# A hybrid decoder trunk: whole blocks ahead of chunk products in linear attention, state updates in one run, and drains of plain sums without a wait for the combined ones

## The chip, the cores and the metric

The kernel runs on one core of a Trainium2 chip. Every time is in device microseconds (us) of that core, from the start to the end of one execution. The engines are named as the profile names them: PE is the matrix engine, PEld its loading of stationary operands, DVE the vector engine, ACT the scalar engine, POOL the general one, and SP the one that here only issues transfers.

## The reference, cut to what matters

Two layers work on 256 tokens of width 2048, all in float32. A layer has a linear-attention group of 8 heads and a stick-breaking group of 8 heads side by side, an output projection, and a squared-ReLU MLP of width 8192.

```
# linear attention, in chunks of 64 tokens: q_e = q exp(b), k_e = k exp(-b), b the summed log gates
scores  = where(causal, q_e k_e^T, 0)          # within a chunk
o_intra = scores v
u       = (k exp(b_last - b))^T v              # one per chunk
state   = decay * state + u                    # over chunks
o_inter = q_e state_before_the_chunk
o_gla   = rms_norm(o_intra + o_inter) * silu(gate)
# the rest of a layer
x = x + concat(o_gla, o_sb) w_o
x = x + square(relu(rms_norm(x) w_up)) w_down
```

## The kernel before, in words

**Products.** A product of float32 operands is made of three faster ones: each operand is split into a high and a low part (`act` for activations, `whi` and `wlo` for weights), and high by high, high by low and low by high are summed (lines 569 to 571, and 1352 to 1354). Weights arrive in tiles `raw` from HBM, ACT writes `whi` (lines 550 and 1239), DVE writes `wlo` (lines 552 and 1243). For two of the eight tiles of an MLP unit the low part is made by ACT and an adding transfer instead (`dlo`, lines 1249 and 1252).

**First half of a layer (projections and attention).** `unit` multiplies one block of 512 projection columns. Small work of the attention heads is hung on the units' steps with `after`: each step of a unit is 12 products, and work due after n steps is issued behind the n-th. The order within this half is then left to the scheduler of the language, which may also set instructions of one engine past each other.

For a pair e of linear-attention heads (4 pairs in each layer) there are two such pieces of work. `gla_pair` (line 988) makes six sums u of three chunks and two heads in one PSUM bank (line 996), four blocks of scores in another (line 1013), the states S of three chunks on DVE (lines 1002 and 1004), and the masked scores (line 1024). Two steps later `gla_out` (line 1031) sums, in one bank, four whole blocks of 128 by 128 (masked scores by values, line 1037) and six chunk products (scaled queries of 64 tokens by the state before the chunk, line 1049). The sums u, the scores and the chunk products have 64 output rows each, the upper or the lower half of the partitions; in the profile they are the matmuls with `128*64`, all others have `128*128`. Each of these plain float32 products stands in the profile as two matmul instructions.

**Second half (output projection and MLP).** From line 1072 on the work of a layer is given to a planner, `Plan`, as pieces with an engine, an assumed length and the pieces that they depend on. PE keeps the order in which pieces are added; a piece of DVE or ACT gets a due time from those who use it, and whichever is ready and due first comes next. What it writes out is the order on PE, DVE and ACT.

A unit of that half is one block of 1024 output columns: 16 times `up` and `down` in turns of two, and two of the output projection, in each layer. Four of its eight weight tiles (two in the output projection) are multiplied in a form with seven block products for eight. So of the eight PSUM banks a unit fills, four (m1, m5, m6, m7) hold sums that are to be combined, and four (m2, m4, m3, m8) hold **plain** sums, which only have to be added to the result. The result is `xb` (the residual stream) in a `down` unit and a tile `act` in an `up` unit. m1, m5, m6 and m7 are complete three steps before the unit's end, m2 and m4 one step before, m3 and m8 at its end. The next unit begins with m2 and m4 (six matmuls each), then m3 and m8.

`down_tail` (line 1360) and `up_tail` (line 1407) add the pieces that drain a unit's banks: `sums` combines the four banks of the first kind, `half` adds the plain banks, m2 and m4 in its first call and m3 and m8 in its second. All of the drains on DVE go through `combine` (line 1080). An `up` unit then goes through ReLU (ACT, line 1438), transposes on PE (line 1456) into m5, m7, m1 and m6, and squares (ACT, line 1463).

## Time and profile before

| what | value |
|---|---|
| median of 3 runs | 2174.51 us (2174.15 to 2175.42) |
| the profiled execution | 2175.34 us, of which the traced span is 2173.2 us |
| PE, busy share of the span | 99% |
| PEld | 82% |
| DVE | 85% |
| ACT | 67% |
| DMA queue with the weights, share of 16 engines | 54.8% |
| granted PE clock | 1.00 |

Matmuls are pipelined: each shows some 0.39 us in the timeline while the next starts 0.23 us later. So a busy PE says little, and costs are read from the distance between two starts. The linear attention stands at about 242 to 300 us in the first layer and 1319 to 1378 us in the second; the planned half at 307 to 1090 us and 1386 us to the end.

### The profile page before, as it was taken

The page shows a single profiled execution, that of the slowest core. Times are in us where ns is not written, and L with a number is a line of the kernel's source. Part 1 is how long each engine was busy: PE and PEld are TensorE (multiplying, and loading weights), DVE is VectorE, ACT ScalarE, POOL GpSimd, SP SyncE. Part 2 cuts the span into 40 slices and gives each one's busy share as a digit, 9 for nine tenths or more (in the row PEclk, how much of TensorE's full clock was granted, in tenths as well). Part 3 has the DMA queues.
Part 4 walks back from the last instruction along what each step waited for, and adds up shares of the span by engine and source line. Part 5 has one row for each costly group of instructions (what it writes and reads, how often), then busy time and mean ns, then how long its engine had stood idle before and what let it go on. Part 6 is the DMA issues. An engine that isn't in the chain of part 4 may idle for free.

```text
span 2173.2 us, 28234 instructions
## 1 busy us (share of the span) xinstructions
PE 2159.4 (99%) x10256; PEld 1784.1 (82%) x10256; DVE 1857.4 (85%) x2469; ACT 1456.6 (67%) x1855; POOL 152.0 (7%) x202
## 2 busy tenths in 40 slices
PE   9999999999999999999999999999999999999999
PEld 7988778888888888888888887788888888888887
DVE  5677569999999999999967775699999999999998
ACT  5555356687677677677745553567776776776775
POOL 0020000000000000000100200000000000000000
PEclk9999999999999999999999999999999999999999
DMA  6655455688888888888746544556888888888885
GB/s 226 193 163 159 155 174 195 196 250 251 249 256 236 262 249 241 260 246 251 230 139 195 173 156 152 195 177 219 247 251 264 234 257 248 246 243 251 258 245 175
DMA packets 171502, 476.15 MB, mean 219 GB/s; under 512 B 9210, under 2 KB 34370, under 8 KB 171364
## 3 DMA queue, kind: packets, MB, share of 16 engines
q1 hardware_dynamic: 152932, 407.24, 54.8%
q0 software_dynamic: 18432, 67.12, 16.4%
q8 instruction: 80, 1.31, 0.2%
q14 instruction: 58, 0.48, 0.1%
HBM read 405.12 MB, written 2.10 MB: 187 GB/s over the span
## 4 chain that ended last, share of the span: by engine, by line
PE 92%; DVE 4%; issue 2%; ACT 1%; DMA 1%; SPq 0%; POOL 0%; ACTq 0%
PE acc L569 6%; PE acc L571 6%; PE acc L570 6%; PE acc L616 3%; DVE act L1080 2%; PE acc L620 1%; DVE wlo L1243 1%; ACT whi L1239 1%; PE ps L1037 1%; PE ps L1049 1%; DMA dlo<-raw 1%; DVE t L1080 0%; PE ps L996 0%; PE ps L732 0%; PE ps L678 0%
## 5 line engine op out<-in xcount | busy, mean ns | idle before, releaser
L1239 ACT ACTIVATE whi<-raw 128x1024 fp32r<-128x1024 f32 x728 | 704.5, 978 | 299.4 <-ACT dlo L1249 29.3
L1243 DVE TENSOR_TENSOR wlo<-raw,whi 128x1024 fp32r<-128x1024 f32 x600 | 653.6, 1099 | 64.8 <-ACT whi L1239 55.9
L552 DVE TENSOR_TENSOR wlo<-raw,whi 128x1024 fp32r<-128x1024 f32 (+2 forms) x194 | 220.5, 1140 | 132.5 <-ACT whi L550 132.3
L550 ACT ACTIVATE whi<-raw 128x1024 fp32r<-128x1024 f32 (+2 forms) x194 | 189.6, 983 | 204.3 <-PE acc L571 154.3
L569 PE MATMUL acc<-whi,act 128*128 128x512 f32 (+2 forms) x640 | 243.0, 380 | 1.3 <-ACT act L471 1.3
L570 PE MATMUL acc<-wlo,act 128*128 128x512 f32 (+2 forms) x640 | 237.8, 372 | 0.0
L571 PE MATMUL acc<-whi,act 128*128 128x512 f32 (+2 forms) x640 | 237.5, 371 | 0.0
L1252 POOL DMA_DIRECT2D dlo<-raw x128 | 110.3, 862 | 1531.3 <-ACT dlo L1249 862.8
L1239 ACT ACTIVATE whi<-ts 128x1024 fp32r<-128x1024 f32 x136 | 144.5, 1062 | 90.7 <-DVE ts L1080 5.1
L1243 DVE TENSOR_TENSOR wlo<-ts,whi 128x1024 fp32r<-128x1024 f32 x136 | 165.9, 1220 | 10.4 <-ACT whi L1239 8.5
L1080 DVE TENSOR_TENSOR ts<-raw 128x1024 f32<-128x1024 f32 x136 | 166.2, 1222 | 2.4
L569 PEld LDWEIGHTS acc<-whi,act 128*128 128x128 f32 x640 | 121.2, 189 | 24.4 <-issue 4.1
L571 PEld LDWEIGHTS acc<-whi,act 128*128 128x128 f32 x640 | 120.8, 189 | 21.4 <-issue 0.7
L570 PEld LDWEIGHTS acc<-wlo,act 128*128 128x128 f32 x640 | 121.1, 189 | 19.0 <-issue 0.7
L1249 ACT ACTIVATE dlo<-raw 128x1024 fp32r<-128x1024 f32 x128 | 133.0, 1043 | 0.0
L1080 DVE TENSOR_TENSOR raw<-raw 128x512 f32<-128x512 f32 x136 | 93.6, 688 | 2.3
L1080 DVE TENSOR_TENSOR raw<-ts,raw 128x512 f32<-128x512 f32 x136 | 93.3, 686 | 0.9
L616 PE MATMUL acc<-act,whi 128*128 128x512 f32 x256 | 91.9, 401 | 0.0
L620 PE MATMUL acc<-act,wlo 128*128 128x256 f32 x256 | 71.8, 280 | 0.0
L616 PEld LDWEIGHTS acc<-act,whi 128*128 128x128 f32 x256 | 48.1, 188 | 11.1
L446 DVE TENSOR_TENSOR act<-t,act 128x512 fp32r<-128x512 f32 x76 | 52.0, 685 | 0.0
L620 PEld LDWEIGHTS acc<-act,wlo 128*128 128x128 f32 x256 | 48.4, 189 | 0.1
(2996 smaller groups left out, 5125.4 us busy)
## 6 DMA issues: line engine op xcount, KB each, us to landing
raw<-in_w_up_dram SPq DMA_DIRECT2D x112, 1024.0 KB, 5.2
raw<-in_w_down_dram SPq DMA_DIRECT2D x112, 1024.0 KB, 5.7
raw<-in_w_in_dram SPq DMA_DIRECT2D x84, 1024.0 KB, 5.1
dlo<-raw POOLq DMA_DIRECT2D x128, 512.0 KB, 5.2
raw<-in_w_o_dram SPq DMA_DIRECT2D x32, 1024.0 KB, 5.0
raw<-in_w_up_dram SPq DMA_DIRECT2D x32, 512.0 KB, 6.1
raw<-in_w_down_dram SPq DMA_DIRECT2D x32, 512.0 KB, 6.6
raw<-in_w_in_dram SPq DMA_DIRECT2D x14, 512.0 KB, 4.2
```

The costliest lines, as they stand in the source:

```text
L550: newest["hi"] = nc.scalar.activation(h, r, AF.Copy).ins
L552: newest["lo"] = nc.vector.tensor_tensor(lo[:, q : q + step, :width], r, f32(h), ALU.subtract).ins
L569: nc.tensor.matmul(o, xh[:, sl], whi[:, j, :width], start=first, stop=False)
L570: nc.tensor.matmul(o, xh[:, sl], wlo[:, j, :width], start=False, stop=False)
L571: st["mm"] = nc.tensor.matmul(o, xl[:, sl], whi[:, j, :width], start=False, stop=last).ins
L616: nc.tensor.matmul(acc[:, f, :], whi[:, j, sl], op.both(k), start=(k == 0), stop=False, skip_group_check=True,)
L620: nc.tensor.matmul(acc[:, f, T:], wlo[:, j, sl], xh, start=False, stop=(k == KT - 1), skip_group_check=True,)
L1080: nc.vector.tensor_tensor(dst, a, b, op)
L1239: nc.scalar.activation(box["h"][:, :n], src(), AF.Copy)
L1243: nc.vector.tensor_tensor(box["l"][:, :n], src(), f32(box["h"][:, :n]), ALU.subtract)
L1249: nc.scalar.activation(box["l"], src(), AF.Copy, scale=-1.0)
L1252: nc.gpsimd.dma_start(f32(box["l"]), src(), accum_op=ALU.add)
```

## The change

**In `gla_pair`** the states are no longer written between the sums u: first all six sums, then the four blocks of scores, then one run of copy and two updates on DVE. **In `gla_out`** the four whole blocks come first, and then the six chunk products, in the order of (head, chunk) (0,3), (0,2), (1,3), (1,2), (0,1), (1,1).

**In `down_tail`** the drain of a plain bank depends on that bank's products alone, and no more on the combined sum that goes to the same part of `xb`; both are additions to it. Those who read `xb` wait for both. In the two units that write the output the old dependence stays. **In `up_tail`** the drain waits for the combined sum of its own part as before, but no more for the last of the combined sums; only the part (0, 1), which that last sum reads, still does.

```diff
         def gla_pair(e, v, vc):
...
-                if n == 0:
-                    nc.vector.tensor_copy(S[:, 0, :], u)
-                else:
-                    nc.vector.scalar_tensor_tensor(
-                        S[:, n, :], S[:, n - 1, :], dec[:, e, n : n + 1], u,
-                        ALU.mult, ALU.add,
-                    )
...
+            nc.vector.tensor_copy(S[:, 0, :], pu[:, :P])
+            for n in (1, 2):
+                nc.vector.scalar_tensor_tensor(
+                    S[:, n, :], S[:, n - 1, :], dec[:, e, n : n + 1],
+                    pu[:, n * P : (n + 1) * P], ALU.mult, ALU.add,
                 )
...
         def gla_out(e, v, vc, S, sc):
             po = ps_tile()
-            first = True
+
+            def out(j, tt):
+                return po[:, (2 * j + tt) * P : (2 * j + tt + 1) * P]
+
             for j in range(2):
                 for tt in range(NT):
-                    o = po[:, (2 * j + tt) * P : (2 * j + tt + 1) * P]
                     nc.tensor.matmul(
-                        o, sc[:, (2 * tt + j) * P : (2 * tt + j + 1) * P],
+                        out(j, tt), sc[:, (2 * tt + j) * P : (2 * tt + j + 1) * P],
                         v[:, tt, vc + j * P : vc + (j + 1) * P],
-                        start=first, stop=False, skip_group_check=True,
+                        start=(j == 0 and tt == 0), stop=False, skip_group_check=True,
                     )
-                    first = False
-                    for half in range(2):
-                        n = 2 * tt + half
-                        if n == 0:
-                            continue
-                        c0 = n * CHUNK
-                        ps = slice(half * CHUNK, (half + 1) * CHUNK)
-                        nc.tensor.matmul(
-                            o[ps, :], qz[e // 2][:, e % 2, j, c0 : c0 + CHUNK], S[:, n - 1, :],
-                            start=False, stop=(half == 1), skip_group_check=True,
-                        )
+            for j, n in ((0, 3), (0, 2), (1, 3), (1, 2), (0, 1), (1, 1)):
+                tt, half = divmod(n, 2)
+                nc.tensor.matmul(
+                    out(j, tt)[half * CHUNK : (half + 1) * CHUNK, :],
+                    qz[e // 2][:, e % 2, j, n * CHUNK : (n + 1) * CHUNK], S[:, n - 1, :],
+                    start=False, stop=True, skip_group_check=True,
+                )
...
-                    free[m] = [add("DVE", V1, fn, p[m], box["s"][2 * c + tt])]
-                    got += free[m]
+                    free[m] = [add("DVE", V1, fn, p[m], box["s"][2 * c + tt] if end else [])]
+                    got += [*free[m], box["s"][2 * c + tt]]
...
-                    a = vector(y(h, tt), bk(m), y(h, tt), p[m], box["s"][2 * h + tt], box["s"][3], op=minus)
+                    before = [box["s"][2 * h + tt]] + [box["s"][3]] * ((h, tt) == (0, 1))
+                    a = vector(y(h, tt), bk(m), y(h, tt), p[m], before, op=minus)
```

On PE, at the first `gla_pair` of a layer (the rows are instructions in PE's order; - is before, + is the change, rows without a sign are in both; L1006 is the line of the scores in the changed kernel):

```order
-L996 MATMUL ps_2266<-v_417_2244,kdz_239 64x128 x2
-L1013 MATMUL ps_2277<-act_1688,act_1807 64x128 x4
+L996 MATMUL ps_2266<-v_417_2244,kdz_239 64x128 x6
+L1006 MATMUL ps_2274<-act_1688,act_1807 64x128 x4
 L569 MATMUL acc_2247<-whi_2287,act_130 128x512
 L570 MATMUL acc_2247<-wlo_2288,act_130 128x512
-L996 MATMUL ps_2266<-v_417_2244,kdz_239 64x128 x2
 L571 MATMUL acc_2247<-whi_2287,act_130 128x512
 L569 MATMUL acc_2247<-whi_2287,act_130 128x512
 L570 MATMUL acc_2247<-wlo_2288,act_130 128x512
 L571 MATMUL acc_2247<-whi_2287,act_130 128x512
-L996 MATMUL ps_2266<-v_417_2244,kdz_239 64x128 x2
```

The ten products with 64 output rows stood in three places, between products of the projection; now they stand in one. At every second pair the three places were two, eight products in the first and two in the second.

On PE, at the `gla_out` of that pair:

```order
-L1037 MATMUL ps_2321<-v_417_2244,t_425_2282 128x128
-L1049 MATMUL ps_2321<-S_2267,act_1688 64x128
-L1037 MATMUL ps_2321<-v_417_2244,t_425_2282 128x128
-L1049 MATMUL ps_2321<-S_2267,act_1688 64x128 x2
-L1037 MATMUL ps_2321<-v_417_2244,t_425_2282 128x128
-L1049 MATMUL ps_2321<-S_2267,act_1688 64x128
-L1037 MATMUL ps_2321<-v_417_2244,t_425_2282 128x128
-L1049 MATMUL ps_2321<-S_2267,act_1688 64x128 x2
+L1039 MATMUL ps_2321<-v_417_2244,t_425_2282 128x128 x4
+L1046 MATMUL ps_2321<-S_2267,act_1688 64x128 x6
```

Whole blocks and chunk products took turns, four runs of each; now there is one run of each. Over the whole program PE has 16 runs of products with 64 output rows, where it had 52; no other instruction of PE, and none of POOL or SP, changes its place.

On DVE, at the end of the second `up` unit of the first layer, before (m2 to m8 are the banks; `act_884` and `act_885` are the two halves of the unit's result, `t2_888` the intermediate sum):

```order
L1080 TENSOR_TENSOR act_884_4442<-m7__833_4206,t2_888_4458 128x512
L1080 TENSOR_TENSOR act_885_4443<-m5__830_4195,t2_888_4458 128x512
L1080 TENSOR_TENSOR act_885_4443<-m5__830_4195,act_884_4442 128x512
L1243 TENSOR_TENSOR wlo_895_4487<-raw2_862_4335,whi_889_4460 128x1024
L1080 TENSOR_TENSOR act_884_4442<-m2__808_4104,act_884_4442 128x512
L1080 TENSOR_TENSOR act_884_4442<-m4__810_4115,act_884_4442 128x512
L1080 TENSOR_TENSOR act_885_4443<-m3__816_4143,act_885_4443 128x512
L1080 TENSOR_TENSOR act_885_4443<-m8__820_4156,act_885_4443 128x512
```

and in the changed kernel, whose lines 1078 and 1241 are the 1080 and 1243 of before:

```order
L1078 TENSOR_TENSOR act_884_4442<-m2__808_4104,act_884_4442 128x512
L1078 TENSOR_TENSOR act_884_4442<-m7__834_4208,t2_888_4458 128x512
L1078 TENSOR_TENSOR act_885_4443<-m5__831_4197,t2_888_4458 128x512
L1078 TENSOR_TENSOR act_885_4443<-m5__831_4197,act_884_4442 128x512
L1078 TENSOR_TENSOR act_885_4443<-m3__816_4142,act_885_4443 128x512
L1078 TENSOR_TENSOR act_884_4442<-m4__810_4116,act_884_4442 128x512
L1078 TENSOR_TENSOR act_885_4443<-m8__820_4156,act_885_4443 128x512
L1241 TENSOR_TENSOR wlo_896_4508<-raw2_862_4335,whi_889_4460 128x1024
```

The drain of m2 has moved from behind the three combined sums and a `wlo` to ahead of them, and that `wlo` stands behind all of the drains. In a `down` unit the drains of m2, m4, m3 and m8 likewise move ahead, and those of m1 and m7 stand behind that of m8. At the end of the second `down` unit of the first layer, seven additions and two `wlo` stood between the drains of m5 and that of m4; in the changed kernel two additions and three `wlo` do.

More of the change, by code (lines that the diff above doesn't have):

```diff
@@ L1032, in gla_out @@
             po = ps_tile()
-            first = True
+            def out(j, tt):
+                return po[:, (2 * j + tt) * P : (2 * j + tt + 1) * P]
             for j in range(2):
                 for tt in range(NT):
-                    o = po[:, (2 * j + tt) * P : (2 * j + tt + 1) * P]
                     nc.tensor.matmul(
-                        o, sc[:, (2 * tt + j) * P : (2 * tt + j + 1) * P],
+                        out(j, tt), sc[:, (2 * tt + j) * P : (2 * tt + j + 1) * P],
                         v[:, tt, vc + j * P : vc + (j + 1) * P],
-                        start=first, stop=False, skip_group_check=True,
+                        start=(j == 0 and tt == 0), stop=False, skip_group_check=True,
                     )
-                    first = False
-                    for half in range(2):
-                        n = 2 * tt + half
-                        if n == 0:
-                            continue
-                        c0 = n * CHUNK
-                        ps = slice(half * CHUNK, (half + 1) * CHUNK)
-                        nc.tensor.matmul(
-                            o[ps, :], qz[e // 2][:, e % 2, j, c0 : c0 + CHUNK], S[:, n - 1, :],
-                            start=False, stop=(half == 1), skip_group_check=True,
-                        )
+            for j, n in ((0, 3), (0, 2), (1, 3), (1, 2), (0, 1), (1, 1)):
[4 more added lines that the diff above has]
+                    start=False, stop=True, skip_group_check=True,
+                )
             if e % 2 == 0:
```

## The prediction

> **What bounds the kernel now.** I read the page first, then the stage of linear attention by windows and by groups, then single starts in the timeline.
>
> ```profile
> PE 2159.4 (99%) x10256; PEld 1784.1 (82%) x10256; DVE 1857.4 (85%) x2469; ACT 1456.6 (67%) x1855; POOL 152.0 (7%) x202
> ```
>
> PE leads, but 99% is not 99% of its speed. The window 242 to 294 us, most of the first layer's linear attention (start, end, length, then busy us of each engine), and two groups of the same window:
>
> ```profile
> 242.00:294.00 52.00, 52.00 (x289) 37.46 (x288) 30.16 (x54) 16.85 (x23) 0.61 (x2) 1.00 0.37 122
> L550 ACT ACTIVATE whi<-raw 128x1024 fp32r<-128x1024 f32 x12 | 12.7, 1059 | 18.1 <-PE acc L571 18.0
> L1024 DVE TENSOR_TENSOR t<-ps,gmask 64x256 f32<-64x256 f32 x8 | 3.3, 417 | 0.1
> L1004 DVE SCALAR_TENSOR_TENSOR S<-S,dec,ps 128x128 f32<-128x128 f32 x8 | 2.8, 346 | 1.2 <-PE ps L996 0.9
> ```
>
> PE shows 52.00 of 52.00 us, yet ACT stood idle 18.0 us because PE had not yet freed a weight buffer, and DVE is busy 30 of 52. The makers of weights are ahead and PE sets the pace, so a microsecond less between PE's starts is one off the end. The Trainium skill (Perfetto Trace Analysis, Identifying the Most-Contended Engine) says that matmul busy time is no measure of headroom and sends the reader to the weight loads; the trace agrees, with 37.46 against 52.00. By matmul busy alone the first two terms below would be nothing and the sum some 14 us higher.
>
> **Term 1: three visits become one.** `gla_pair` before, on PE (start, length, x2 for one plain product):
>
> ```profile
> 241.93 0.39 PE L571 MATMUL acc<-whi,act 128*128 128x512 f32 x1
> 242.25 0.44 PE L996 MATMUL ps<-v,kdz 128*64 128x128 f32 x4
> 242.52 0.61 PE L1013 MATMUL ps<-act,act 128*64 128x128 f32 x8
> 243.05 0.50 PE L569 MATMUL acc<-whi,act 128*128 128x512 f32 x1
> 243.39 0.40 PE L570 MATMUL acc<-wlo,act 128*128 128x512 f32 x1
> 243.72 0.44 PE L996 MATMUL ps<-v,kdz 128*64 128x128 f32 x4
> 244.08 0.50 PE L571 MATMUL acc<-whi,act 128*128 128x512 f32 x1
> 244.42 0.40 PE L569 MATMUL acc<-whi,act 128*128 128x512 f32 x1
> ...
> 255.50 0.39 PE L571 MATMUL acc<-whi,act 128*128 128x512 f32 x1
> ...
> 257.58 0.40 PE L570 MATMUL acc<-wlo,act 128*128 128x512 f32 x1
> ```
>
> A projection product starts 0.23 after the one before it where nothing intervenes (249.61 to 249.84, below). Into a visit it is 0.32 (241.93 to 242.25): 0.09 for going over to 64 rows. Two products take 0.27 at the head of a visit (242.25 to 242.52) and 0.36 when they are all of it (243.72 to 244.08), so the way out costs 0.09. Four products and the way out take 0.53 (242.52 to 243.05), so a product is (0.53 - 0.09) / 4 = 0.11, and the first two carry 0.05 more. The first projection product afterwards takes 0.34 (243.05 to 243.39): 0.11 more than 0.23.
>
> Visit one costs 243.39 - 241.93 - 2 x 0.23 = 1.00, visit two 244.42 - 243.39 - 2 x 0.23 = 0.57, the third the same: 2.14. One visit of ten products: 0.09 + 0.27 + 8 x 0.11 + 0.09 + 0.11 = 1.44. Gain 0.70. Every second pair has two visits: 257.58 - 255.50 - 0.46 = 1.62, and 0.57, together 2.19; gain 0.75. Four pairs of each kind in two layers: **5.8 us**.
>
> The run on DVE is a copy (at most the 0.35 of an update), two updates of 0.35 and two masked scores of 0.42: under 1.9 us, with one `wlo` of 1.14 (below) between. PE reaches `gla_out` 28 projection products later, after 28 x 0.23 = 6.4 us. That cover hides it; without it, what exceeds 6.4 us would be added at each of 8 places.
>
> **Term 2: blocks and chunk products in one run each.** `gla_out` before, and two rows of the stick-breaking group for plain 128-row products in a row:
>
> ```profile
> 249.61 0.40 PE L571 MATMUL acc<-whi,act 128*128 128x512 f32 x1
> 249.84 0.39 PE L1037 MATMUL ps<-v,t 128*128 128x128 f32 x2
> 250.16 0.43 PE L1049 MATMUL ps<-S,act 128*64 128x128 f32 x2
> 250.52 0.49 PE L1037 MATMUL ps<-v,t 128*128 128x128 f32 x2
> 250.94 0.44 PE L1049 MATMUL ps<-S,act 128*64 128x128 f32 x4
> 251.31 0.49 PE L1037 MATMUL ps<-v,t 128*128 128x128 f32 x2
> ...
> 252.88 0.50 PE L569 MATMUL acc<-whi,act 128*128 128x512 f32 x1
> 253.22 0.40 PE L570 MATMUL acc<-wlo,act 128*128 128x512 f32 x1
> ```
>
> ```profile
> 105.28 0.39 PE L750 MATMUL ps<-v,hA 128*128 128x128 f32 x2
> 105.50 0.39 PE L744 MATMUL ps<-v,hA 128*128 128x128 f32 x2
> ```
>
> Before: 253.22 - 249.84 - 0.23 = 3.15. A block costs 0.22 in a row (105.28 to 105.50), 0.32 ahead of chunk products (249.84 to 250.16), so 0.10 for going over, and 0.42 between two visits (250.52 to 250.94). A lone chunk product takes 0.36 (250.16 to 250.52), a pair in opposite halves 0.37 (250.94 to 251.31). So the pair runs side by side, and a lone one costs 0.36 - 0.05 - 0.09 = 0.22. The new order has two pairs, then two of one half, which I price as lone: 4 x 0.22 + 0.10 + 0.05 + 2 x 0.22 + 2 x 0.22 + 0.10 + 0.11 = 2.12. Gain 1.03, at 8 places **8.2 us**.
>
> For terms 1 and 2 the bounds are 36 removed visits at 0.09 + 0.11 for in and out alone (7.2 us), and 36 whole two-product visits less the products, 0.57 - 0.22 + 0.10 for the block's restart (16 us). I take 14.0 since each run is built from its own rows.
>
> **Term 3: the end of an `up` unit.** PE, and DVE at the same place (the bank names m__808, m__810 are m2, m4 of the ending unit, m__897 m2 of the next):
>
> ```profile
> 499.72 0.39 PE L1354 MATMUL m__820_4156<-whi,act 128*128 128x512 f32 x1
> 500.40 0.47 PE L1352 MATMUL m__897_4500<-whi,act 128*128 128x512 f32 x1 [0.29 <-DVE act L1080]
> 500.70 0.39 PE L1353 MATMUL m__897_4500<-wlo,act 128*128 128x512 f32 x1
> ```
>
> ```profile
> 496.64 0.68 DVE L1080 TENSOR_TENSOR act<-m__833_4206,t 128x512 f32<-128x512 f32 x1
> 497.24 0.68 DVE L1080 TENSOR_TENSOR act<-m__830_4195,t 128x512 f32<-128x512 f32 x1
> ...
> 498.43 1.22 DVE L1243 TENSOR_TENSOR wlo<-raw,whi 128x1024 fp32r<-128x1024 f32 x1
> 499.57 0.68 DVE L1080 TENSOR_TENSOR act<-m__808_4104,act 128x512 f32<-128x512 f32 x1
> ```
>
> ```profile
> PE m__897_4500 L1352 <- DVE act L1080: 0.3, 1, 0.3
> ...
> PE m__3697_17896 L1352 <- DVE act L1080: 0.3, 1, 0.3
> ```
>
> PE should have gone on at 499.95; it started at 500.40, when m2's drain (499.57) was done, and the product after that came 0.30 later: 0.45 + 0.07 = 0.52. The list of waits has 14 such rows, of which these are the first in time and one of the last layer. In the new order m2's drain takes the place at 496.64, and the three sums move by the 0.60 from one drain to the next (496.64 to 497.24), to end about 499.0. Late next would be m4's drain: m3's now stands before it, then m4's from about 499.65 to 500.3, and PE wants m4 six products after 499.95, at 501.3. So the stall goes, with 1 us to spare: 14 x 0.52 = **7.3 us**; bounds 0 (another drain takes its place) and 7.3.
>
> The `wlo` that stood at 498.43 moves behind the drains, to about 500.9, and lands 2.4 us later. It is the third weight of the next unit, first read here:
>
> ```profile
> 507.66 0.48 PE L1352 MATMUL m__897_4500<-whi,act 128*128 128x512 f32 x1
> ```
>
> It is done at about 502.0, over 5 us ahead. That margin and the transposes before it are the cover; without them each such place costs 2.4.
>
> **Term 4: the end of a `down` unit ahead of an `up` unit.**
>
> ```profile
> 585.05 0.39 PE L1354 MATMUL m__1049_5225<-whi,act 128*128 128x512 f32 x1
> 585.42 0.50 PE L1352 MATMUL m__1052_5238<-whi,act 128*128 128x512 f32 x1
> 585.76 0.39 PE L1353 MATMUL m__1052_5238<-wlo,act 128*128 128x512 f32 x1
> ```
>
> ```profile
> PEld m__1364_6694 L1352 <- DVE xb L1080: 0.4, 1, 0.4
> ...
> PEld m__3315_16115 L1352 <- DVE xb L1080: 0.4, 1, 0.4
> ```
>
> Here m4 was late: 0.37 + 0.34 - 2 x 0.23 = 0.25, at 6 places: **1.5 us**, bounds 0 and 1.5. Behind the drains of m5, seven additions and two `wlo` stood ahead of m4's drain, 7 x 0.60 + 2 x 1.14 = 6.5; now two and three, 4.6: 1.9 earlier, where 0.25 is enough. The drains of m1 and m7 come later, behind m8's, which waits for the unit's last product; they end some 3 us after it (m8's and three more additions of 0.60, with a `wlo` at most between). The next unit wants m7 only after 30 products of 0.23, which is 6.9 us, and m1 after 36. The remaining edits change no instruction's cost and I put them at nothing: all that moves is 0.60 us additions, between the weights' work on DVE.
>
> **Sum.** 5.8 + 8.2 + 7.3 + 1.5 = 22.8 us off the profiled execution of 2175.34 us: 2152.5. The median of the runs is 0.83 lower (2174.51), so **2151.7 us**.
>
> **The rivals.**
>
> A. *The stall at the unit's end moves to another bank.* For: on DVE one drain that waits for PE holds all behind it, and m3's, done by PE late, now precedes m4's. Against: the 1 us to spare. Terms 3 and 4 are lost: 2151.7 + 8.8 = 2160.5.
>
> B. *PE waits in `gla_out` for the states.* They are now finished after the scores, and the chunk product that comes first reads the last state. For: DVE had to wait for L996 already (0.9 us in the group's row). Against: 6.4 us of cover for some 3 of work. If term 2 is eaten: 2159.9.
>
> C. *Slower: weights behind drains.* At an `up` unit's end four drains now stand in front of a `wlo`, and the last of them waits for the unit's last product. If the reader of that `wlo` were near, each of 14 places would lose up to 2.4 us, 33.6 in all, against 22.8 gained: 2185.3. It decides from 22.8 / 14 = 1.6 us per place on. Against: the 5 us of margin above.
>
> D. *Nothing.* If another resource, such as the transfers, set the pace, PE's shorter visits would turn into waits: 2174.5. Against: ACT's idle 18.0 us, which PE's products ended.
>
> **How the numbers follow.** My forecast 0.72, with its own range 2148.4 to 2155.7 (below, the 16 us bound of terms 1 and 2, 2.0, and the 1.3 by which the runs shown spread; above, 4 us lost among the terms); A 0.12; B 0.08; C 0.04; D 0.04. The range 2148 to 2163 takes in the forecast, A and B and leaves out C, D and a tail. A change below 0.2% (4.3 us) can't be told from none with this kernel. A, B and the forecast are faster than that: 0.92; D is the same: 0.04; C slower: 0.04.
>
> **What would show it right or wrong.** In the changed profile the products of `gla_pair` should stand in one run, some 1.2 us from its first start to the next projection product, and `gla_out` should take about 2.2 us from its first block to the second projection product less 0.23, rather than 3.15. The 14 waits of PE and 6 of PEld on DVE at the first product of a bank should be gone, and the distance across an `up` unit's end should be 0.23. It is wrong if the chunk products' starts stay as far apart in one run as now, if PE shows a wait for S, or if a wait for `wlo` or for a drain of m3, m4 or m8 appears where m2's was.

## The result and the profile after

The changed kernel takes **2151.94 us** (median of its runs, 2150.99 to 2153.97) where the kernel before takes 2174.40 us beside it (2174.15 to 2175.42). The ratio is 0.9897, with a 95% interval from 0.988 to 0.9914. The forecast was 2151.7 us, with a range from 2148 to 2163. The profiled execution took 2150.99 us, of which 2149.1 us are the traced span; before it was 2175.34 and 2173.2.

In the code of the changed kernel the lines 1080, 1239, 1243, 1249, 1252 and 1352 to 1354 of before are 1078, 1237, 1241, 1247, 1250 and 1350 to 1352; the scores of `gla_pair` are line 1006, the whole blocks and the chunk products of `gla_out` 1039 and 1046.

The first part of the page after, and the window 242 to 294 us (start, end, length, then busy us of PE, PEld, DVE, ACT and POOL):

```profile
PE 2137.9 (99%) x10256; PEld 1783.4 (83%) x10256; DVE 1855.6 (86%) x2469; ACT 1448.0 (67%) x1855; POOL 152.0 (7%) x202
```

```profile
242.00:294.00 52.00, 52.00 (x318) 42.40 (x315) 31.09 (x58) 17.11 (x26) 0.61 (x2) 1.00 0.49 164
```

PE still shows 99%, and 52.00 of 52.00 us in the window, but it now gets 318 matmuls into it where it got 289. Only the loading of weights shows it: 42.40 us busy where it was 37.46.

`gla_pair` and `gla_out` of the first pair, in the timeline of PE after:

```profile
240.80 0.39 PE L571 MATMUL acc<-whi,act 128*128 128x512 f32 x1
241.12 0.88 PE L996 MATMUL ps<-v,kdz 128*64 128x128 f32 x12
241.82 0.61 PE L1006 MATMUL ps<-act,act 128*64 128x128 f32 x8
...
242.69 0.39 PE L570 MATMUL acc<-wlo,act 128*128 128x512 f32 x1
...
247.94 1.06 PE L1039 MATMUL ps<-v,t 128*128 128x128 f32 x8
248.93 1.09 PE L1046 MATMUL ps<-S,act 128*64 128x128 f32 x12
...
250.28 0.39 PE L570 MATMUL acc<-wlo,act 128*128 128x512 f32 x1
```

The three visits of `gla_pair` are one. Its price is 242.69 - 240.80 - 2 x 0.23 = 1.43 us; it was 2.14 and forecast at 1.44. `gla_out` takes 250.28 - 247.94 - 0.23 = 2.11 us; it was 3.15 and forecast at 2.12.

The end of the first `up` unit after, on PE and on DVE (m__808, m__810 and m__820 are m2, m4 and m8 of the ending unit, m__895 and m__898 are m2 and m4 of the next):

```profile
492.12 0.39 PE L1352 MATMUL m__820_4156<-whi,act 128*128 128x512 f32 x1
492.34 0.39 PE L1350 MATMUL m__895_4499<-whi,act 128*128 128x512 f32 x1
...
493.70 0.39 PE L1350 MATMUL m__898_4512<-whi,act 128*128 128x512 f32 x1
```

```profile
489.03 0.69 DVE L1078 TENSOR_TENSOR act<-m__808_4104,act 128x512 f32<-128x512 f32 x1
...
492.02 0.69 DVE L1078 TENSOR_TENSOR act<-m__810_4116,act 128x512 f32<-128x512 f32 x1
...
493.21 1.22 DVE L1241 TENSOR_TENSOR wlo<-raw,whi 128x1024 fp32r<-128x1024 f32 x1
```

PE goes over in 0.22 us where it took 0.68. The drain of m2 stands ahead of the sums; that of m4 ends at 492.71, 1.0 us before PE wants the bank at 493.70. The `wlo` behind the drains starts 0.87 us after the crossing, where it started 1.52 us before it would have been: 2.4 us later. All three numbers are those of the forecast.

Three rows of PE's list of waits after (us in total, times, longest us):

```profile
PE m__2487_12187 L1351 <- DVE wlo L1241: 0.8, 1, 0.8
PE m__536_2766 L1351 <- DVE wlo L1241: 0.8, 1, 0.8
...
PE m__3870_18694 L1350 <- DVE xb L1078: 0.2, 1, 0.2
```

The 14 rows on a drain of m2 and the 6 rows of PEld are gone. These three were not in the list before, and the forecast had none of them; nor had it a fourth, 0.2 us of PE for a `whi` ahead of the first product of the planned half in the second layer (m__2487).

**Where the 24 us went.** I set the start of each PE product outside `gla_pair` and `gla_out` beside the start of the same product in the other trace. The difference is a shift, and a step in it is a place where time was won or lost. This ledger is used for all the runs below.

| place | won or lost, us | forecast |
|---|---|---|
| first 14 us of the kernel | +1.1 | none |
| linear attention, layer 1 and layer 2 | +7.2, +7.2 | 14.0 in both |
| start of the planned half, layer 1 and layer 2 | -0.7, -1.2 | none |
| 14 ends of `up` units, 0.53 each | +7.4 | 7.3 |
| 6 ends of `down` units ahead of `up`, 0.27 each | +1.6 | 1.5 |
| small steps, mostly of 0.01 to 0.04, behind these ends | +0.8 | none |
| last unit: bank m__3870 | -0.46 | none |
| last unit: transfer of `dlo` | +1.46 | none |
| from the last product to the end of the span | -0.3 | none |
| sum | 24.1 | 22.8 |

The first row is no work of the change (the last section shows what is known of it). Without it the two traces differ by 23.0 us.

The loss at the start of the planned half is this, on PE, on SP's queue and on ACT, after:

```profile
296.36 0.40 PE L1350 MATMUL m__536_2766<-whi,act 128*128 128x512 f32 x1
297.51 0.50 PE L1351 MATMUL m__536_2766<-wlo,act 128*128 128x512 f32 x1 [0.75 <-DVE wlo L1241]
```

```profile
286.09 0.37 SPq L1210 DMA_DIRECT2D raw<-in_w_o_dram  x1
286.55 3.67 SPq L1210 DMA_DIRECT2D raw<-in_w_in_dram  x2
```

```profile
295.13 1.06 ACT L1237 ACTIVATE whi<-raw 128x1024 fp32r<-128x1024 f32 x1 [1.46 <-DMA raw<-in_w_in_dram]
```

and the same transfer, its reader on ACT and the first product of the planned half before:

```profile
293.46 0.42 SPq L1212 DMA_DIRECT2D raw<-in_w_in_dram  x1
```

```profile
301.91 1.04 ACT L1239 ACTIVATE whi<-raw 128x1024 fp32r<-128x1024 f32 x1
```

```profile
304.66 0.39 PE L1352 MATMUL m__536_2766<-whi,act 128*128 128x512 f32 x1
```

PE reaches the planned half 304.66 - 296.36 = 8.3 us earlier than before, but the weight that it wants next was sent for only 293.46 - 286.55 = 6.9 us earlier, and takes 8.5 us to the start of its `whi` in both. The 1.4 us between the two were more than the slack that there was. So a part of what PE won was given back to a transfer.

### The profile page after: what moved, and what is told of

It is laid out like the page before. It is cut to its first block, busy times and chain, and to the rows that moved or that the text cites. A ratio compares the mean times of both kernels' runs of the same rounds, so it can differ in the third digit from the quotient of the medians.

```text
span 2149.1 us, 28267 instructions
## 1 busy us (share of the span) xinstructions
PE 2137.9 (99%) x10256; PEld 1783.4 (83%) x10256; DVE 1855.6 (86%) x2469; ACT 1448.0 (67%) x1855; POOL 152.0 (7%) x202
## 4 chain that ended last, share of the span: by engine, by line
PE 96%; DVE 2%; DMA 1%; issue 0%; ACT 0%; SPq 0%; POOL 0%; DVEq 0%
PE acc L569 6%; PE acc L571 5%; PE acc L570 5%; PE acc L616 3%; PE acc L620 1%; DMA raw<-in_w_in_dram 1%; DVE wlo L552 0%; PE ps L732 0%; DVE xb L1078 0%; PE ps L678 0%; PE ps L696 0%; PE ps L1046 0%; PE ps L1039 0%; DVE wlo L1241 0%; PE ps L996 0%
## 5 line engine op out<-in xcount | busy, mean ns | idle before, releaser
L1437 ACT ACTIVATE act<-act,st 128x512 f32<-128x512 f32 x64 | 43.9, 712 | 18.8 <-DVE act L1078 18.8
```

## The experiments

The times stand beside the kernel before on the same chip, and the ratio is to it; the changed kernel's own is 0.9897.

| run | median, us | before, us | ratio, 95% interval |
|---|---|---|---|
| out_alone | 2166.91 | 2173.76 | 0.9968 (0.9955 to 0.9981) |
| pair_alone | 2167.45 | 2173.76 | 0.9970 (0.9958 to 0.9981) |
| gla_alone | 2162.57 | 2173.76 | 0.9947 (0.9930 to 0.9963) |
| tails_alone | 2163.70 | 2173.76 | 0.9950 (0.9936 to 0.9965) |
| up_alone | 2167.84 | 2174.36 | 0.9970 (0.9959 to 0.9982) |
| down_alone | 2172.52 | 2174.36 | 0.9991 (0.9981 to 1.0000) |
| one_half | 2150.84 | 2174.36 | 0.9893 (0.9878 to 0.9908) |
| early_load | 2148.52 | 2174.36 | 0.9880 (0.9863 to 0.9896) |
| changed_again | 2151.94 | 2174.51 | 0.9897 (0.9882 to 0.9912) |
| joined | 2146.89 | 2174.51 | 0.9875 (0.9859 to 0.9892) |
| end_free | 2149.88 | 2174.51 | 0.9889 (0.9874 to 0.9904) |
| best | 2147.92 | 2174.51 | 0.9878 (0.9864 to 0.9893) |

**Each edit of linear attention alone.** On the kernel before, only `gla_out`'s new order:

```diff
+            for j, n in ((0, 3), (0, 2), (1, 3), (1, 2), (0, 1), (1, 1)):
...
-                    for half in range(2):
```

> Only the new order of gla_out (whole blocks in one run, then the chunk products), everything else as before. Theory (each run costs what its starts cost, term 2): each of the 8 places shorter by 1.04 us, 8.3 in all, as the changed kernel showed beside the pair's edit; of that, part comes back where the planned half begins and PE reaches a weight whose transfer PE itself released: the changed kernel gave back 0.7 and 1.2 us at the two layers for a gain of 7.2 in each, and with a gain of about 4.1 per layer I expect 0.4 to 1.2 back in sum. Time 2174.4 - 8.3 + 0.8 = 2166.9. Rival 1 (the place gains only together with gla_pair's edit, since the states are made after the scores there): under 4 us, 2170 or more. Rival 2 (a visit costs nothing beside its products): no change, 2174.4. Profile: PE's places in gla_out take 2.1 us from the first block to the second projection product less 0.23, gla_pair still three visits of 2.14 in sum.

By the ledger the eight places win 1.01 to 1.07 us each, 8.2 in all, as forecast (8.2). Layer 1 gives 0.04 us back at the start of the planned half and layer 2 gives 1.10. Both rivals fall: the gain needs no help from the other edit, and a visit does cost something beside its products.

Only `gla_pair`'s:

```diff
-                if n == 0:
-                    nc.vector.tensor_copy(S[:, 0, :], u)
...
+            nc.vector.tensor_copy(S[:, 0, :], pu[:, :P])
```

> Only gla_pair's edit (the copy and the two updates of the states behind the scores, so that the state products and the score products of a pair are emitted together), gla_out as before. Theory (term 1): 0.73 to 0.77 us off at each of 8 pairs, 5.8 to 6.1 in all, less 0.3 to 0.9 given back at the start of the two planned halves: 2174.4 - 5.9 + 0.6 = 2169.1. Rival 1 (the states are now ready too late for gla_out's first chunk product, which stands only one block behind its start in this order): the gain turns into waits of PE at the chunk products of gla_out, 2172 or more. Rival 2 (the gain is that of fewer visits to 64-row products whatever the stage): this edit removes 12 visits and the changed kernel as a whole 36 for 14.4 us, 0.40 each, so 4.8 us: 2169.6 less what is given back.

By the ledger each pair wins 0.77 to 0.78 us, 6.2 in all, and 0.05 and 0.59 are given back. Rival 1 falls: no wait of PE for S stands in the trace. Rival 2's 4.8 is below what was measured: a removed visit was not worth the same everywhere, 12 of them giving 6.2 us here and 24 giving 8.2 in `gla_out`. Term 1 was 0.4 us too small in sum. The single visit costs what I said (1.43), but the projection products that follow a visit start 0.230 to 0.236 us apart for a while, instead of 0.227, and two fewer visits mean less of that; the rest of the 0.06 per pair is there.

Both:

> Both edits of linear attention, the ends of the planned units as before. Theory (the terms add and the ends have no part in it): 7.2 us shorter in each layer's linear attention, 14.4 in all, and 1.9 given back where the planned half begins, both as in the changed kernel: 2174.4 - 14.4 + 1.9 = 2161.9. Rival (the give-back belongs to the new ends of the units or to the last unit, not to linear attention): 2160.0. Rival (the two edits do not add, because gla_pair's later states meet gla_out's chunk products): over 2164. Profile: the wait of PE for wlo at the first steps of the planned half is there with 1.1 to 1.3 us, as in the changed kernel, and the 14 waits of PE and 6 of PEld on DVE at the units' ends are there as before.

The ledger has 7.19 and 7.22 us, so the two edits add (8.2 + 6.2 = 14.4). It has 0.52 and 0.87 given back, 1.4 rather than 1.9, with the wait of PE for `wlo` in layer 2's list, 0.8 us, as in the changed kernel. So the loss at the start of the planned half belongs to linear attention and not to the units' ends.

**Each edit of the units' ends alone.** Both, with linear attention as before:

> Both edits of the ends of the planned units, linear attention as before. Theory (terms 3 and 4): 14 x 0.53 = 7.4 and 6 x 0.27 = 1.6, 9.0 in sum: 2174.4 - 9.0 = 2165.4, and up to 1.0 less if the wait for the last unit's transfer goes as it did in the changed kernel. Rival (the drains are late only when measured against a PE that waits there for another reason, so the stall moves): 2172 or more, with rows of PE waiting on DVE at other banks. Rival (weights behind drains): a wait for wlo at the third weight of a unit, up to 2.4 us at each of 14 places: slower than 2174. Profile: none of the 14 waits of PE at L1352 and 6 of PEld on DVE is left, and the planned half starts as before, with 0.5 us or less at its first product.

By the ledger 9.9 us are won at the 20 ends, the small steps among them; 0.46 is lost at the bank m__3870 and 1.45 won at the last transfer of `dlo`. None of the 20 waits is left. Theory held, and the two unforeseen items in the last unit belong to these edits.

Only `up_tail`:

```diff
-                    a = vector(y(h, tt), bk(m), y(h, tt), p[m], box["s"][2 * h + tt], box["s"][3], op=minus)
+                    before = [box["s"][2 * h + tt]] + [box["s"][3]] * ((h, tt) == (0, 1))
+                    a = vector(y(h, tt), bk(m), y(h, tt), p[m], before, op=minus)
```

> Only the edit of the drains at an up unit's end (a plain bank's drain no longer waits for the unit's other sums), the rest as before. Theory (term 3): 14 ends at 0.53 us: 7.4 off, and 14 to 20 small steps of 0.04 behind them; the last unit, whose transfer PE waited 1.2 us for before, gains 0 to 1.3 more. Time 2173.8 - 7.4 - 0.6 = 2165.8. Rival (the up ends gain only because the down ends ahead of them gained too): less than 5 us, 2169 or more. Profile: none of the 14 waits of PE at L1352 on the drain is left, the 6 of PEld on xb are there.

The median lies 6.5 us below before where 8.0 were expected, and the ledger does not show the 14 gains alone. All 14 are there, 0.53 each, 7.4 in sum, and 8 new losses of 0.46 each, 3.7 in sum. One of the eight in the list of waits:

```profile
PE m__983_4902 L1352 <- DVE xb L1080: 0.2, 1, 0.2
```

The first of these places, on PE and on DVE (m__898 is m4 of the ending `down` unit, m__983 the m4 of the `down` unit that follows):

```profile
542.67 0.39 PE L1354 MATMUL m__981_4890<-whi,act 128*128 128x512 f32 x1
543.28 0.50 PE L1352 MATMUL m__983_4902<-whi,act 128*128 128x512 f32 x1 [0.23 <-DVE xb L1080]
```

```profile
540.21 1.22 DVE L1243 TENSOR_TENSOR wlo<-raw,whi 128x1024 fp32r<-128x1024 f32 x1
...
542.54 0.68 DVE L1080 TENSOR_TENSOR xb<-m__898_4512,xb 128x512 f32<-128x512 f32 x1
```

and in the kernel before:

```profile
544.48 0.39 PE L1352 MATMUL m__983_4903<-whi,act 128*128 128x512 f32 x1
```

```profile
543.59 0.68 DVE L1080 TENSOR_TENSOR xb<-m__898_4510,xb 128x512 f32<-128x512 f32 x1
...
544.78 1.22 DVE L1243 TENSOR_TENSOR wlo<-raw,whi 128x1024 fp32r<-128x1024 f32 x1
```

Before, the drain of m4 at the end of a `down` unit ahead of another `down` unit was done at 544.27, 0.2 us before PE wanted the bank. With `up_tail` alone PE came 1.6 us earlier, and the drain 1.05 us earlier, since a `wlo` that stood behind it now stands ahead of it. The rival named for this run is not what happened (the `up` ends gain by themselves); what happened is rival A of the forecast, at another kind of end than the one I looked at. One more loss in this trace, 0.33 us at 1299 us in the second layer's attention, stands in no other, and its cause stays open.

Only `down_tail`:

```diff
-                    free[m] = [add("DVE", V1, fn, p[m], box["s"][2 * c + tt])]
-                    got += free[m]
+                    free[m] = [add("DVE", V1, fn, p[m], box["s"][2 * c + tt] if end else [])]
+                    got += [*free[m], box["s"][2 * c + tt]]
```

> Only the edit of the additions at a down unit's end, the rest as before. Theory (term 4): 6 ends at 0.27 us: 1.6 off, 2172.2, with 0 to 1.3 more at the last unit's transfer if that depends on how the drains of the last units stand. Rival (the stall is given on to the next bank): 2173.8. Profile: the 6 waits of PEld on xb gone, the 14 waits of PE on the drains of m2 there as before with 0.3 each.

The ledger has 6 x 0.28 = 1.7 us won and 0.3 lost at the last `dlo`; the median is 1.8 below before, with an interval that reaches 1.0000, so here the ledger and not the median bears the reading. The theory held for this run. Alone the two edits are worth 3.7 and 1.7 at the ends, together 9.4 (9.9 less the 0.46 at m__3870): the down edit earns 4 us more beside the up edit than alone. Of that 3.2 come from seven of the eight places, where it brings the drain of m4 forward too (the eighth, m__3870, is in the last unit, which keeps the old dependence), and the rest from the small steps, which hardly show with either edit alone.

**Do opposite halves run side by side?** The changed kernel with the chunk products ordered by half:

```diff
-            for j, n in ((0, 3), (0, 2), (1, 3), (1, 2), (0, 1), (1, 1)):
+            for j, n in ((0, 3), (1, 3), (0, 1), (1, 1), (0, 2), (1, 2)):
```

> The changed kernel with gla_out's chunk products in another order: (0,3), (1,3), (0,1), (1,1), (0,2), (1,2) instead of (0,3), (0,2), (1,3), (1,2), (0,1), (1,1), so that neighbours lie in the same half of the rows and only one step changes the half; the same products, the same visits, the same output. Theory (products in opposite halves run side by side, two in one half behind one another, 0.22 for a lone one): the changed order had two pairs and two lone ones, 4 times 0.22; this one has five or six separate ones, 5 to 6 times 0.22 less what a change of half saves, so 0.22 to 0.44 per place longer, 1.8 to 3.5 us over 8 places: 2153.7 to 2155.4 where the changed kernel has 2151.9. Rival (a chunk product costs the same wherever it lies and the old order's 0.36 and 0.37 were the visits alone): no difference, 2151.9. Profile: the eight places' distance from the first block to the second projection product behind longer by 0.22 to 0.44, or not.

The first place:

```profile
246.70 1.06 PE L1039 MATMUL ps<-v,t 128*128 128x128 f32 x8
247.69 1.15 PE L1046 MATMUL ps<-S,act 128*64 128x128 f32 x12
...
249.10 0.40 PE L570 MATMUL acc<-wlo,act 128*128 128x512 f32 x1
```

It takes 249.10 - 246.70 - 0.23 = 2.17 us, 0.06 more than in the changed kernel; the ledger has 0.05 per place, 0.4 in all. (The median is lower than the changed kernel's, but this trace is 1.2 us ahead of the other before linear attention begins, so the median does not show the order's price.) Theory and rival both fail by their numbers (0.22 to 0.44, and nothing). The starts of the twelve instructions say why. In ns from the first block product:

```
changed kernel   987  993 1147 1154 1256 1263 1365 1372 1474 1583 1692 1802
one_half         987 1147 1256 1365 1474 1480 1583 1641 1693 1750 1802 1859
```

In both, one sequence goes on at 109 ns: 987, 1147, 1256, 1365, 1474, 1583, 1692, 1802. These are the eight instructions of the four products of the upper half (chunks 1 and 3). In the changed kernel the four of the lower half start 6 to 7 ns beside the first four. In the other order they come last in the program, yet the first of them starts at 1480, when the upper half still has three of its eight to start. The trace doesn't name the half of an instruction; I read it from the spacing and the order in the program. So the halves do run side by side, as the forecast had it; but a product needs no partner next to it, since one half's instructions start while earlier ones of the other still wait. A run ends with the half that ends last: the upper one in the changed kernel (1802), the lower one here (1859), and these 57 ns are the 0.06 us. My pricing of the last two products as "lone" gave the right number for that reason.

**Is the transfer the cause of what was given back?** The changed kernel with the two buffers that it borrows from linear attention dealt out to other weights:

```diff
-                if x % RAWS in (0, 2):
+                if x % RAWS in (2, 4):
```

> The changed kernel with the buffers of the planned half's first raw weights dealt out otherwise: the loads that reuse room of linear attention (and so wait for PE's last whole blocks of gla_out) are the third and fifth of each round of buffers instead of the first and third, so that the first two loads of the planned half are free to be issued early. Nothing computed changes. Theory (what was given back at the start of the planned half, 0.7 and 1.2 us, is the time of a transfer that PE's own progress releases, 8.6 us from issue to landing): the waits of 1.15 and 1.26 us in front of the first unit's second product go, 0.3 to 0.4 per layer may stay one step later, where the wait of before was; about 1.4 us off: 2150.5 where the changed kernel has 2151.9. Rival (the weight is late because DVE comes to it late, behind the states and scores of the last pair): no difference, the waits of 1.15 and 1.26 us remain. Rival (the load that is gated in its stead is late too, a few products on): the waits move, no difference in time.

PE, SP's queue and ACT at the start of the planned half:

```profile
296.24 0.39 PE L1350 MATMUL m__536_2766<-whi,act 128*128 128x512 f32 x1
296.47 0.39 PE L1351 MATMUL m__536_2766<-wlo,act 128*128 128x512 f32 x1
```

```profile
285.98 0.92 SPq L1210 DMA_DIRECT2D raw<-in_w_in_dram  x2
289.74 10.06 SPq L1210 DMA_DIRECT2D raw<-in_w_o_dram  x2
```

```profile
291.25 1.05 ACT L1237 ACTIVATE whi<-raw 128x1024 fp32r<-128x1024 f32 x1
```

The two waits are gone, and by the ledger 0.67 and 1.17 us are won, 1.8 in all: all of what was given back, and more than the 1.4 expected. The rivals of a late DVE and of a wait that only moves expected no difference, and fall. The mechanism is not quite the one I wrote. The burst of loads goes out at the same time as before (285.98 and 286.09 us), but the two of the unit that PE needs first now go ahead of the output projection's instead of behind, and the first `whi` starts 5.3 us after its load instead of 8.6. So it is shown that the place of these loads in the burst decides the loss. That PE itself releases the burst is not. SP's list of waits of the changed kernel, between 270 and 300 us, has:

```profile
SPq L1210 <- DVE wlo L552: 14.2, 2, 8.9
...
SPq L1210 <- PE ps L1039: 2.9, 1, 2.9
```

The wait of 8.9 us ends at the first load of the burst (286.09), and is put down to DVE's last `wlo` of linear attention; the one of 2.9 us for PE stands only ahead of the third load, at 289.85. So a part of the theory fails: PE holds back one load and not the burst. What sets the time of the burst was not taken away by any run.

**Fewer visits still, and the last units.** First the changed kernel itself again, as a measure:

> The changed kernel itself once more, as the measure for the other three on the same chip: 2151 to 2152.5, with the waits of 1.15 and 1.26 us in front of the second product of the planned half and the wait of 0.39 us at the bank m__3870 of the last unit.

It took 2151.94 us. The bank m__3870 is as in the first trace, but the waits at the start of the planned half are not where I expected them. In the first layer 0.78 us lie between the first two products instead of 1.15; in the second PE waits 0.69 us for a `whi` ahead of the first product (0.22 in the first trace), and 1.26 lie between the two as before. By the ledger the layers give back 0.3 and 1.6 us, where the first trace has 0.7 and 1.2: the sum is the same, 1.9, but one layer's share moves by 0.4 between two executions of one program, and the shares above are no better known than that. The first 14 us differ too: this execution is 1.0 us ahead there and stays ahead.

Then the early load together with two edits: chunk products first in `gla_out`, and the second pair one step (12 products) earlier, so that its `gla_pair` runs into the first pair's `gla_out`:

```diff
-                after(1 + 3 * hp, lambda e=2 * g + hp, v=v, c=hp * 2 * P: gla_pair(e, v, c))
+                after(1 + 2 * hp, lambda e=2 * g + hp, v=v, c=hp * 2 * P: gla_pair(e, v, c))
```

> The early load of the run before it, and linear attention put in still fewer visits: gla_out's chunk products go first and its whole blocks last, and the second pair of a group comes one projection product earlier, so that its gla_pair ends where the first pair's gla_out begins and both are one visit to 64-row products (12 visits in the whole kernel instead of 16; the same products, the same sums in another order). Theory (a visit costs its way in and its way out, 0.09 to 0.11 and 0.20 to 0.22 us with the slower first product behind it): 4 visits less at 0.3 us, 1.2, and with the load's 1.8 together 3.0 us off the changed kernel. Rival 1 (the chunk products now come first and wait for the states): PE waits for S at up to 4 places, the gain of the visits is gone. Rival 2 (a visit's price lies in the first and last product of a run only, whichever their rows): no gain beside the load's 1.8. Profile: the sums of the starts, place by place.

One of the four joined places (here line 1039 is the chunk products and 1046 the whole blocks):

```profile
246.64 0.88 PE L996 MATMUL ps<-v,kdz 128*64 128x128 f32 x12
247.35 0.61 PE L1006 MATMUL ps<-act,act 128*64 128x128 f32 x8
247.78 1.04 PE L1039 MATMUL ps<-S,act 128*64 128x128 f32 x12
248.76 1.16 PE L1046 MATMUL ps<-v,t 128*128 128x128 f32 x8
249.67 0.48 PE L569 MATMUL acc<-whi,act 128*128 128x512 f32 x1
```

The four visits less win 0.42 us each, 1.7 in all (1.2 expected: the way in and out of 64 rows, and the slower restart of the projection, fall away together with a little of the pace behind them), the load 1.9. No wait for S is in the trace, and nothing is given back at the start of the planned half: both rivals fall. By the ledger the kernel is 3.6 us ahead of the changed one, where 3.0 were expected; the median is 2146.89 us.

Then the drains of the last two `down` units freed as well:

```diff
-                    free[m] = [add("DVE", V1, fn, p[m], box["s"][2 * c + tt] if end else [])]
+                    free[m] = [add("DVE", V1, fn, p[m])]
```

with the store of the output moved behind the later of a part's two additions.

> The changed kernel, with the drains of the last two down units freed of their unit's other sums as all the others already are; the output's transfer goes out behind whichever of a half's two additions comes last. The same additions in another order. Theory (PE waits 0.46 us at m__3870 only because the last down units keep the old dependence): that wait goes, 0.4 to 0.5 us off by the starts, too little for the clock on the wall. Rival 1 (the stall is DVE's weight in front of the drains, whatever they wait for): it stays. Rival 2 (the plan of the last units moves and the transfer of dlo is waited for again as in the kernel before): 1.0 to 1.5 us longer at 2136.

The wait is gone; after, and here:

```profile
2104.19 0.39 PE L1352 MATMUL m__3868_18680<-whi,act 128*128 128x512 f32 x1
2104.81 0.50 PE L1350 MATMUL m__3870_18694<-whi,act 128*128 128x512 f32 x1 [0.23 <-DVE xb L1078]
```

```profile
2103.25 0.39 PE L1352 MATMUL m__3869_18680<-whi,act 128*128 128x512 f32 x1
2103.47 0.39 PE L1350 MATMUL m__3872_18692<-whi,act 128*128 128x512 f32 x1
```

That is 0.47 us, and `dlo` is not waited for. So the loss at m__3870 was the same stall as the eight of up_alone, in the last of the eight units, which the down edit left out.

Last, all three:

> All three together on the changed kernel: the early load (1.8 us), the joined visits (1.2 us) and the freed drains of the last down units (0.45 us). Theory (they lie in different places and add): 3.4 us less than the changed kernel on the same chip, about 2148.4 where that takes 2151.8. Rival (what PE gains in linear attention is again taken back at the start of the planned half by the next transfer): under 2 us.

By the ledger 1.7 + 1.9 + 0.5 = 4.1 us less than the changed kernel's trace, of which each part is where it was alone, and nothing is given back. The medians are 2147.92 here and 2146.89 for joined. A difference of 0.05% between them can't be told by the medians. Of the two traces joined's is 0.9 us shorter, but it is 1.4 us ahead before linear attention begins; behind that point best is 0.5 ahead, the freed drains.

## Why the prediction was right, point by point

**What bounds the kernel.** Right. A microsecond less between PE's starts was a microsecond off the end at nearly every place, and the terms were won where the forecast put them. The Trainium skill's rule (Perfetto Trace Analysis, Identifying the Most-Contended Engine), that matmul busy time says nothing of headroom and the weight loads do, is borne out by the change itself: in the window of 52 us the matmuls stayed at 52.00 us and the weight loads went from 37.46 to 42.40.

**Term 1** (5.8 us): 6.2 measured. The visit is as priced (1.43 for 1.44); missing was the slower pace of the products behind each visit.

**Term 2** (8.2): 8.2 measured. The prices hold; the pairing of neighbours behind one of them is not how PE does it, as one_half shows, but with four products in one half and two in the other it gives the same sum.

**Term 3** (7.3): 7.4 measured, with the margin of 1 us at m4 that the forecast named. But the step "late next would be m4's drain" was followed at the `up` unit's own end only. At the next kind of end, a `down` unit ahead of a `down` unit, the trace of before had 0.2 us to spare. Without the down edit 3.7 of the 7.4 us are lost there.

**Term 4** (1.5): 1.6 measured. Beside the up edit it is worth some 4 us more, mostly because it clears seven of those eight places. The sum of the two terms was right since the two edits came together, not because each does what I priced.

**The edits put at nothing.** Here the working failed. "The makers of weights are ahead and PE sets the pace" was read from one window in the middle of linear attention. At its end the makers were ahead by less than the gain, and 1.9 us were given back; gla_alone and early_load show whose they are and why. The last unit kept its old dependence and lost 0.46 us, which end_free shows. The plan of the last unit moved, which won 1.46 us; that the order in the plan is the cause is read from two traces, and no run moved this transfer alone. Before, in the timeline of ACT and of PE:

```profile
2126.76 1.06 ACT L1239 ACTIVATE whi<-raw 128x1024 fp32r<-128x1024 f32 x1 [0.71 <-PE m__3795_18340 L1354]
2127.73 1.04 ACT L1249 ACTIVATE dlo<-raw 128x1024 fp32r<-128x1024 f32 x1
```

```profile
2136.07 0.39 PE L1352 MATMUL m__3867_18681<-whi,act 128*128 128x512 f32 x1
2137.64 0.50 PE L1353 MATMUL m__3867_18681<-dlo,act 128*128 128x512 f32 x1 [1.18 <-DMA dlo<-raw]
```

and ACT in tails_alone:

```profile
2116.86 1.06 ACT L1249 ACTIVATE dlo<-raw 128x1024 fp32r<-128x1024 f32 x1 [0.42 <-PE m__3795_18340 L1353]
```

Before, the part that becomes `dlo` was made behind a `whi`, 8.6 us ahead of the read that was due at 2136.30; in tails_alone it is made ahead of that `whi`, 10.3 us ahead of the same read (2127.16), and the transfer is there in time. In every run with the up edit the wait is gone, and in every run without it some of it is left.

**The sum.** -1.9, -0.46, +1.46, +0.8 of small steps and -0.3 at the end nearly cancel, and the first 14 us of the kernel, which differ from one execution to the next, are worth 1.1 us between the two traces. So it is luck that forecast and median lie only 0.2 us apart: what the forecast left out was of the size of 2 us each way.

**The rivals.** A (the stall moves) did not happen at the 20 ends of the whole change, but did in the last unit, at m__3870, and happens at eight places with the up edit alone. B (waits for the states) did not happen, even where chunk products came first. The cover against it was smaller than forecast: PE has 24 products between the scores and `gla_out` and not 28, 5.6 us (242.36 to 247.94). It was enough, since DVE had finished the states and masked scores at 244.82. C (weights behind drains) did not: the `wlo` came the forecast 2.4 us later, and no wait for it at an `up` unit's end stands in the list. D (another resource takes the gain) happened on a small scale, 1.9 of 14.4 us, at the start of the planned half of each layer, where a transfer was due.

## What to carry to other kernels

When PE sets the pace and one stage is made faster, look at the end of that stage and not at its middle: compare how much earlier PE arrives at the next stage with how much earlier the next weights are sent for. When a stall is removed at one kind of boundary, read the margin at every other kind of boundary that follows it, since 0.2 us to spare were used up here by the 0.5 us won one unit earlier. And products of half height are cheapest in one visit, with each visit to them between full products worth 0.3 to 0.5 us here.

## What the runs showed of the hardware

By the starts of one_half and the changed kernel, products into opposite halves of the 128 rows run in two sequences of their own, each 109 ns from start to start behind its first (160 ns), and one started while three earlier instructions of the other had not; in these two orders neither order nor adjacency mattered by more than 0.06 us. Going over between products with 64 and with 128 output rows costs 0.09 to 0.11 us each way, and the first 512-column product behind a visit another 0.11.

The first projection products of the kernel start at different times in different executions of the same kernel:

```profile
8.78 0.50 PE L569 MATMUL acc<-whi,act 128*128 128x512 f32 x1 [1.31 <-ACT act L471]
```

```profile
7.80 0.48 PE L569 MATMUL acc<-whi,act 128*128 128x512 f32 x1
```

The first row is from the changed kernel's trace and the second from changed_again's, the same program twice. The shift is 1.0 us then and stays so for the whole linear attention; the spans of the two, 2149.1 and 2148.2 us, differ by about as much. Against the kernel before's trace the others are between 0.3 us behind (tails_alone) and 2.5 us ahead (joined) when linear attention begins.

Two things go into this. The first projection product starts at 8.7 to 8.9 us in seven of the 14 traces, the kernel before's and the changed kernel's among them, and at 7.5 to 7.8 us in the others; the cause of that was not tried. And the pace is not the same: in the kernel before the products from 9.48 to 13.34 us start 0.43 us apart and the later ones 0.23, in tails_alone it is 0.43 up to 13.78 us, and in changed_again it is 0.23 from 8.12 us on, but for one wait for a weight. The record of the granted clock in these traces begins to show 1.00 at 13.3, 14.0 and 7.8 us. In the changed kernel's first trace it does so at 7.2 us, so the +1.1 us at the head of the ledger is mostly the moment at which the clock was granted, and not the change. What share of the spread of a kernel's runs this makes can't be said, since one execution of each run is traced.
